# Moving softmax scaling, gate evictions and first taps between VectorE and ScalarE, and taking the recurrence's gates as a tangent of half the value, in a hybrid decoder step

## The chip, the core and the metric

The kernel runs on one core of a Trainium2 chip. Its engines are TensorE (PE, with its weight loads shown as PEld), VectorE (DVE), ScalarE (ACT), GpSimd (POOL) and SyncE (SP), which here issues the DMAs. The metric is device microseconds of one execution; the kernel before takes 1209.53 us (median of three runs, 1209.03 to 1210.03).

## The reference

One step of a hybrid decoder layer, for 1024 prompt tokens and 8 x 4 sample tokens, in float32. One input projection gives the columns of two groups. The recurrent group (RG-LRU, 512 features) goes through a convolution of width 4 over time, two block-diagonal gates and a linear recurrence; the attention group has 8 query heads and 2 key heads of width 64, a window of 128 and a learned sink per head. Both are normed, joined, projected, added to the input and layer-normed; a SwiGLU feed-forward (2816 wide) and a second layer norm follow.

```python
r = sigmoid(einsum(xb, w_a) + b_a);  i = sigmoid(einsum(xb, w_x) + b_x)
log_a = -8 * r * softplus(-lru_lambda)
a = exp(log_a)
u = sqrt(-expm1(2 * log_a)) * (i * x)
h = a * h + u                                  # over time
m = max(max(s), sink);  p = exp(s - m);  p = p / (sum(p) + exp(sink - m))
y_lru = gelu(gate) * lru_out
```

## The kernel before

All activations lie feature-major: 128 features on the partitions, tokens along the free axis, in two chunks of 512 and 544 tokens (the second is the last 512 prompt tokens and the 32 sample tokens, worked in two blocks of 272). Every float32 operand of a projection is split into a high and a low part, and a product takes three passes on TensorE (`three`, line 589).

The instructions are not issued in the order in which they are written. A recorder (`Recorder`) collects them, and a list scheduler (`order`, line 261) issues them per engine by the latest start that would not hold up TensorE, with a cost for each instruction worked out from its shape (`cost`, line 428). An instruction given to `either` may go to one of two engines: the first named does it if that is in time, otherwise the one that is through with it first (`leave`, line 313). `tt` (line 207) is such a choice between GpSimd and VectorE, `copy` (line 213) between ScalarE and VectorE. A function that needs another activation table than the one loaded is put back for a while (PATIENCE, line 62). All recorded instructions are issued from line 417, so the profile tells them apart by the names of their tiles.

The tiles that matter here:
- `attend` (line 849): one block of 128 queries for two heads. TensorE makes scores s; VectorE adds the mask and takes the minimum (p<-s,mk,ng); ScalarE takes the exponential of p with its sum in st; VectorE takes the reciprocal of st and scales p by it; TensorE transposes p into tp; ScalarE (or VectorE) copies tp to ph and VectorE makes the rest pl; TensorE multiplies with the values into o; ot and yat put the result together. `attend_sample` (line 905) does the same for the sample tokens, with pc for p.
- `recurrence` (line 1046): four taps over xr (and xe, the sample tokens) give xc; ps_g are the two gates' sums, which VectorE evicts to zz with the bias b_a or b_x.
- `scans` (line 1077): sigmoids of zz, then with L = -8 softplus(-lambda) r a tangent and an exponential; the products on zz, xc and hs; a square root; the scan over time into hs.
- `gate_stream` (line 1127): the gate branch; ps_gt is evicted to gt by VectorE.

The stages: up to about 42 us the loads and the first keys; to 473 us input projection, attention, recurrence, norms and output projection side by side, the projections filling TensorE between the steps of the other work; to 1190 us the feed-forward; then the last layer norm.

Of the kernel before, what the change touches and what calls it, by code (L numbers as in the profile page):

```python
# [12 lines left out]
F32 = mybir.dt.float32  # L13
# [39 lines left out]
# ---- a small list scheduler: the kernel below records its instructions; they are issued in the order in which they  # L53
# can run, given what each engine costs per instruction (shapes only), the data they wait for and the free buffers
# [9 lines left out]
TABLES = {"Sigmoid": "sigmoid", "Sqrt": "sqrt", "Gelu_apprx_tanh": "gelu", "Silu": "silu", "Exp": "exp"}  # L64


class RecordPool:
    """a tile pool whose tiles are made when their first instruction is issued; one opened late waits until all tiles
    of `behind` are done with"""
# [17 lines left out]
class Tag:  # L87
    def __init__(self, pool, kind, cap):
        self.pool, self.kind, self.cap, self.psum = pool, kind, cap, pool.psum
        self.bufs, self.free, self.first = [], cap, 0  # L90

# [58 lines left out]
class Recorder:  # L150
# [5 lines left out]
    def add(self, engine, fn, args, kw, *others):  # L156
        """`others`: (engine, function, args, kw) of instructions that would do the same on another engine"""
# [46 lines left out]
    def either(self, *calls):  # L204
        """an instruction that any of several engines can do: the one that would be through with it first"""
        self.add(*calls[0], *calls[1:])
# [9 lines left out]
    @contextlib.contextmanager  # L216
    def batch(self):
        """instructions that are to run one after the other: each waits for the data of all"""
        self.group = []
        yield  # L220
        waits = set().union(*(op.before for op in self.group)) - set(self.group)
        for op in self.group:
            op.before |= waits
        self.group = None

    def extra(self, b):
        """how many buffers the instructions recorded before b's may still need beside those in use"""
        t = b.tag
        ev = []
        for c in t.bufs[t.first : b.order]:  # L230
            if not c.taken:
                ev.append((c.start, 1))
                ev.append((c.end + 0.5, -1))
        ev.sort()
        n = peak = 0
        for _, d in ev:
            n += d
            peak = max(peak, n)
        return peak

    def deadlines(self):
        """op.key: the latest start that does not hold up the tensor engine, were it to run without a gap in the order
        of recording"""
# [19 lines left out]
    def order(self):  # L263
# [41 lines left out]
        def finish(op, e):  # L305
            """when engine e would be through with op after the more urgent work that waits for it"""
# [17 lines left out]
        def dispatch(e):  # L324
# [34 lines left out]
            for b in op.bufs:  # L359
                if not b.taken:  # L360
                    b.taken = True
                    t = b.tag
                    t.free -= 1
                    while t.first < len(t.bufs) and t.bufs[t.first].taken:
# [63 lines left out]
def cost(engine, fn, outs, ins, args, kw):  # L428
    """ns of an instruction, from its shape"""
# [23 lines left out]
def hybrid_step(ctx: ExitStack, tc: tile.TileContext, xT, w_in, w_gates, w_out, w_g, w_u, w_d, vec, ck, cv, ck_nat,  # L453
# [30 lines left out]
    # ---- constants and small vectors  # L484
# [13 lines left out]
    # ---- emission: a queue of matrix work fills the tensor engine between the steps of the other work  # L498
# [16 lines left out]
    def run_filler(stream, step):  # L515
        """emit the stream; after each `step` ns of its matmuls advance the other work"""
# [7 lines left out]
    # ---- weights: a unit is [128, 1024], split exactly into two float32r parts, prefetched in order of use  # L524
# [6 lines left out]
    def load(j):  # L531
        """raw halves of unit j"""
# [9 lines left out]
    def split_unit(j):  # L542
        if state["part"] == j and j < len(units):
# [9 lines left out]
            if halves:  # L553
                # less each row's mean over its columns: the second layer norm would take it off their sums
# [15 lines left out]
    def need(i):  # L570
        """unit i; at its first use the next unit is split and the one after that loaded"""
# [17 lines left out]
    def three(ps, n, wh, wl, xh, xl, start, stop):  # L589
        """(wh + wl).T @ (xh + xl) in three float32r passes"""  # L590
# [5 lines left out]
    def block(ps, u, xs, o, n, kts=range(KT)):  # L596
        """one [128, n] block of a projection: unit u against feature-major activations xs"""
# [7 lines left out]
    # ---- start: the first tokens and the key and value weights arrive and are split tile by tile  # L605
    def wake():
        """while the first loads are on their way: the exponential's table, and the tensor engine's clock"""
# [76 lines left out]
    # 8 * softplus(-lambda) = 8 * (max(-lambda, 0) + log1p(exp(-|lambda|))), the log1p by its atanh series  # L684
    sp = const.tile([P, 8, 4], F32, tag="sp", name="sp")
    lam = vec_cols("lam", 0, 4)
    e_, s_, s2, poly, sp8, nsp8, ab, _ = (sp[:, i] for i in range(8))
# [4 lines left out]
    bcen = ng2[:, 0:8]  # L692
    def small_vectors():
        # b_out less its mean over the features
# [7 lines left out]
        # -sink for the running minimum, and the query bias with the (negated) attention scale  # L702
# [16 lines left out]
        nc.vector.scalar_tensor_tensor(sp8, poly, 2.0, ab, op0=ALU.mult, op1=ALU.add)  # L719
        nc.vector.tensor_scalar(sp8, sp8, 8.0, None, op0=ALU.mult)  # L720
        nc.vector.tensor_scalar(nsp8, sp8, -1.0, None, op0=ALU.mult)

    # ---- rotary embedding
# [7 lines left out]
    # ---- keys and values of token chunk s  # L731
# [4 lines left out]
    def key_stack(g, s, kraw):  # L736
        """[k; k] of a key group, in two float32r parts"""
# [810 lines left out]
```

## Time and profile before

| | us |
|---|---|
| median of the runs | 1209.53 |
| profiled execution, first to last instruction (span) | 1207.1 |
| TensorE busy | 1147.1 (95%) |
| VectorE busy | 631.5 (52%) |
| ScalarE busy | 431.3 (36%) |
| GpSimd busy | 491.1 (41%) |

The page gives for the profiled execution its span; the median of the runs stands 2.4 us above it. The shares are means over the stages named above, which differ: they are to be read stage by stage. Busy time of one engine can overlap at the seams of two instructions; a wait is put down to the instruction that ended it.

### The profile page before, as it was taken

How to read it: one execution, taken by the hardware profiler on the slowest of the kernel's cores; microseconds unless marked ns; L12 is line 12 of the kernel's file. 1: busy time of each engine (PE TensorE's matmuls, PEld its weight loads, DVE VectorE, ACT ScalarE, POOL GpSimd, SP SyncE). 2: the span in 40 equal slices, each digit the busy share in tenths (PEclk: the TensorE clock that was granted, in tenths of full speed). 3: DMA queues.
4: the chain of work that ended last, by engine and by line, in shares of the span. 5: the costliest groups of instructions: out<-in, count | busy, mean ns of one | idle time of the engine just before them, and what ended most of it. 6: DMA issues, size and time to landing. Idle time of an engine off the chain costs nothing.

```text
span 1207.1 us, 18093 instructions
## 1 busy us (share of the span) xinstructions
PE 1147.1 (95%) x7024; PEld 1023.9 (85%) x7024; DVE 631.5 (52%) x1259; ACT 431.3 (36%) x878; POOL 491.1 (41%) x493
## 2 busy tenths in 40 slices
PE   9788998788888999999999999999999999999996
PEld 7568898776668979999898998989999899999986
DVE  5999889899977577252324142232415132232135
ACT  5375666567545375311120212113021211202135
POOL 6843476666556978412031222203031221303241
PEclk9899999899989999999999999999999999999998
DMA  8410113243121223211011111111111110202004
GB/s 291 136 53 19 41 49 101 65 142 117 63 89 54 80 78 129 90 36 53 26 63 35 53 53 45 44 36 53 36 65 41 53 44 27 70 19 70 1 1 144
DMA packets 48085, 80.42 MB, mean 67 GB/s; under 512 B 8144, under 2 KB 12400, under 8 KB 47984
## 3 DMA queue, kind: packets, MB, share of 16 engines
q1 hardware_dynamic: 48000, 79.27, 19.8%
q8 instruction: 55, 0.90, 0.3%
q14 instruction: 30, 0.25, 0.1%
HBM read 71.98 MB, written 5.58 MB: 64 GB/s over the span
## 4 chain that ended last, share of the span: by engine, by line
PE 73%; DVE 17%; DMA 3%; issue 2%; ACT 2%; POOL 2%; SPq 1%; DVEq 0%; POOLq 0%; ACTq 0%
PE ps_d L417 21%; PE ps_fg L417 20%; PE ps_fu L417 20%; PE ps_o L417 4%; DVE p L417 3%; PE ps_gt L417 3%; DVE xc L417 2%; DVE y L417 1%; DVE yat L417 1%; DVE qst L417 1%; SPq L417 1%; DVE hs L417 1%; DVE pl L417 1%; DMA x_r<-in_dram 1%; DVE v L417 1%
## 5 line engine op out<-in xcount | busy, mean ns | idle before, releaser
L417 POOL TENSOR_TENSOR wg_l<-wg_r,wg_h 128x512 fp32r<-128x512 f32 x50 | 64.8, 1311 | 344.4 <-ACT wg_h L417 344.4
L417 DVE SCALAR_TENSOR_TENSOR y<-y,ps_d 128x272 f32<-128x272 f32 (+1 forms) x240 | 124.9, 521 | 107.2 <-PE ps_d L417 102.5
L417 PE MATMUL ps_fg<-h_h,wg_l 128*128 128x272 f32 (+1 forms) x528 | 171.7, 325 | 0.4 <-POOL wg_l L417 0.4
L417 PE MATMUL ps_fg<-h_h,wg_h 128*128 128x272 f32 (+1 forms) x528 | 171.6, 325 | 0.0
L417 PE MATMUL ps_fg<-h_l,wg_h 128*128 128x272 f32 (+1 forms) x528 | 171.4, 325 | 0.0
L417 PE MATMUL ps_d<-hid_h,wd_l 128*128 128x272 f32 (+1 forms) x528 | 171.3, 325 | 0.0
L417 DVE TENSOR_REDUCE wd_c<-wd_r 128x1 f32<-128x512 f32 x44 | 30.0, 682 | 269.3 <-DMA wd_r<-in_dram 269.3
L417 PE MATMUL ps_fu<-h_h,wu_l 128*128 128x272 f32 (+1 forms) x528 | 170.7, 323 | 0.0
L417 PE MATMUL ps_fu<-h_h,wu_h 128*128 128x272 f32 (+1 forms) x528 | 170.6, 323 | 0.0
L417 PE MATMUL ps_d<-hid_h,wd_h 128*128 128x272 f32 (+1 forms) x528 | 170.6, 324 | 0.0
L417 PE MATMUL ps_d<-hid_l,wd_h 128*128 128x272 f32 (+1 forms) x528 | 170.4, 324 | 0.0
L417 PE MATMUL ps_fu<-h_l,wu_h 128*128 128x272 f32 (+1 forms) x528 | 170.4, 323 | 0.0
L417 POOL TENSOR_TENSOR hid_l<-sg,hid_h 128x272 fp32r<-128x272 f32 (+1 forms) x66 | 63.3, 960 | 126.0 <-ACT hid_h L417 108.3
L417 ACT ACTIVATE sg<-ps_fg 128x272 f32<-128x272 f32 (+1 forms) x66 | 30.5, 463 | 232.4 <-PE ps_fg L417 232.4
L417 PEld LDWEIGHTS ps_fg<-h_h,wg_l 128*128 128x128 f32 x528 | 99.8, 189 | 8.5 <-POOL wg_l L417 0.6
L417 PEld LDWEIGHTS ps_fg<-h_l,wg_h 128*128 128x128 f32 x528 | 99.5, 189 | 7.9
L417 PEld LDWEIGHTS ps_fg<-h_h,wg_h 128*128 128x128 f32 x528 | 99.8, 189 | 7.7
L417 PEld LDWEIGHTS ps_d<-hid_h,wd_l 128*128 128x128 f32 x528 | 99.2, 188 | 8.2 <-issue 0.2
L417 PEld LDWEIGHTS ps_d<-hid_h,wd_h 128*128 128x128 f32 x528 | 99.2, 188 | 8.0 <-issue 0.2
L417 PEld LDWEIGHTS ps_fu<-h_l,wu_h 128*128 128x128 f32 x528 | 99.3, 188 | 7.8
L417 PEld LDWEIGHTS ps_d<-hid_l,wd_h 128*128 128x128 f32 x528 | 99.2, 188 | 7.9
L417 PEld LDWEIGHTS ps_fu<-h_h,wu_l 128*128 128x128 f32 x528 | 99.3, 188 | 7.7
(346 smaller groups left out, 2553.1 us busy)
## 6 DMA issues: line engine op xcount, KB each, us to landing
wg_r<-in_dram SPq DMA_DIRECT2D x50, 256.0 KB, 2.6
wu_r<-in_dram SPq DMA_DIRECT2D x50, 256.0 KB, 2.6
wd_r<-in_dram SPq DMA_DIRECT2D x44, 256.0 KB, 2.6
wo_r<-in_dram SPq DMA_DIRECT2D x32, 256.0 KB, 2.6
wq_r<-in_dram SPq DMA_DIRECT2D x16, 256.0 KB, 3.6
wx_r<-in_dram SPq DMA_DIRECT2D x12, 256.0 KB, 3.5
x_r<-in_dram SPq DMA_DIRECT2D x8, 272.0 KB, 4.6
y<-in_dram SPq DMA_DIRECT2D x8, 272.0 KB, 3.4
```

What stands on the lines that cost most here:

```text
L417: getattr(getattr(self.nc, op.eng), op.fn)(*[real(a) for a in op.args], **{k: real(v) for k, v in op.kw.items()})
```

## The change

Five edits, all ahead of the feed-forward:
- The scaling of p and pc by the reciprocal becomes a choice: ScalarE first, VectorE otherwise (`scaled`).
- The first tap of the convolution, and the eviction of ps_gt, become such a choice too.
- The two gates are evicted from PSUM by ScalarE as tanh(x/2 + b/2), with halved biases hb. As sigmoid(x) = (1 + tanh(x/2)) / 2, the separate sigmoids go; tangent and exponential of L take their missing half from a bias, with 4 softplus in place of 8.
- i * x becomes (i' + 1) * x in one VectorE instruction, where it was a product that GpSimd or VectorE could do, and the missing factor 1/2 goes into the square root as scale 0.25.
- u * sqrt(...) now names GpSimd first where it named VectorE first. The table list gets Tanh under "exp", so that the scheduler counts a tangent as belonging to the exponential's table.

The remaining lines of the diff rewrite `extra` to the same result and drop comments. The core:

```diff
-TABLES = {"Sigmoid": "sigmoid", ..., "Silu": "silu", "Exp": "exp"}
+TABLES = {"Sigmoid": "sigmoid", ..., "Silu": "silu", "Exp": "exp", "Tanh": "exp"}
...
+        nc.vector.tensor_scalar(hbias, vec_cols("b_a", 0, 8), 0.5, None, op0=ALU.mult)
...
+    def scaled(p, r):
+        nc.either(("scalar", "activation", (p, p, AF.Identity), dict(scale=r)),
+                  ("vector", "tensor_scalar", (p, p, r, None), dict(op0=ALU.mult)))
...
-            nc.vector.tensor_scalar(pr[:, j, 8 : 8 + w], pr[:, j, 8 : 8 + w], st[:, 4 + j : 5 + j], None, op0=ALU.mult)
+            scaled(pr[:, j, 8 : 8 + w], st[:, 4 + j : 5 + j])
...
-            nc.vector.tensor_scalar(pc[i], pc[i], st[:, 7:8], None, op0=ALU.mult)
+            scaled(pc[i], st[:, 7:8])
...
-            nc.vector.tensor_scalar(dst, src(0), tap[0], col("conv_b", j), op0=ALU.mult, op1=ALU.add)
+            nc.either(("scalar", "activation", (dst, src(0), AF.Identity), dict(scale=tap[0], bias=col("conv_b", j))),
+                      ("vector", "tensor_scalar", (dst, src(0), tap[0], col("conv_b", j)),
+                       dict(op0=ALU.mult, op1=ALU.add)))
...
-                nc.vector.tensor_scalar(zz[q][:, o : o + m], ps[:, :m], col(bias, j), None, op0=ALU.add)
+                nc.scalar.activation(zz[q][:, o : o + m], ps[:, :m], AF.Tanh, bias=hbias[:, 4 * q + j : 4 * q + j + 1],
+                                     scale=0.5)
...
-        with nc.batch():
-            for i in items:
-                nc.scalar.activation(gr[i], gr[i], AF.Sigmoid)
-                nc.scalar.activation(gi[i], gi[i], AF.Sigmoid)
...
-            nc.scalar.activation(t2[i], gr[i], AF.Tanh, scale=sp8[:, i[0] : i[0] + 1])
-        for i in items:
-            nc.tt(gi[i], gi[i], cut(xcs[i], i[1]), op=ALU.mult)
-            nc.scalar.activation(gr[i], gr[i], AF.Exp, scale=nsp8[:, i[0] : i[0] + 1])
+            c = slice(i[0], i[0] + 1)
+            nc.scalar.activation(t2[i], gr[i], AF.Tanh, scale=sp4[:, c], bias=sp4[:, c])
+            nc.scalar.activation(gr[i], gr[i], AF.Exp, scale=nsp4[:, c], bias=nsp4[:, c])
+            nc.vector.scalar_tensor_tensor(gi[i], gi[i], 1.0, cut(xcs[i], i[1]), op0=ALU.add, op1=ALU.mult)
...
-                nc.scalar.activation(t2[i], t2[i], AF.Sqrt)
+                nc.scalar.activation(t2[i], t2[i], AF.Sqrt, scale=0.25)
...
-            nc.tt(u, u, h, op=ALU.mult, first="vector")
+            nc.tt(u, u, h, op=ALU.mult)
...
-                nc.vector.tensor_scalar(graw[j, s][:, o : o + n], ps[:, :n], col("b_in", 4 + j), None, op0=ALU.add)
+                g = graw[j, s][:, o : o + n]
+                nc.either(("scalar", "activation", (g, ps[:, :n], AF.Identity), dict(bias=col("b_in", 4 + j))),
+                          ("vector", "tensor_scalar", (g, ps[:, :n], col("b_in", 4 + j), None), dict(op0=ALU.add)))
```

As the costs and choices feed the scheduler, instructions move on every engine. Two places show it. In names such as p_1_0 the first number is the query tile and the second the block; ISA is VectorE's mask-and-minimum or the read of its result.

VectorE, at blocks 0_3 to 1_1 of the first chunk, before:

```order
L417 RECIPROCAL st_0_3_795<-st_0_3_795 128x2
L417 TENSOR_SCALAR p_0_3_365<-p_0_3_365,st_0_3_795 128x256 x2
L417 TENSOR_TENSOR yat00_766<-o_0_2_846,ot_0_2_868 64x128 x2
L417 RECIPROCAL st_1_0_844<-st_1_0_844 128x2
L417 ISA p_1_1_761,st_1_1_896<-s_1_1_876,mk_272,ng_257 128x256
L417 ISA st_1_1_896 128x1
L417 TENSOR_SCALAR p_1_0_712<-p_1_0_712,st_1_0_844 128x128 x2
```

The same engine and blocks, now:

```order
L418 RECIPROCAL st_1_0_855<-st_1_0_855 128x2
L418 TENSOR_TENSOR pl_0_3_898<-tp_0_3_871,ph_0_3_887 128x512
L418 TENSOR_TENSOR qst40_894<-q20raw_727,qst40_894 64x512
L418 SCALAR_TENSOR_TENSOR hs10_683<-xc10_584,hs10_683 128x512
L418 ISA p_1_1_765,st_1_1_928<-s_1_1_905,mk_274,ng_257 128x256
L418 ISA st_1_1_928 128x1
```

The four scalings have left this stretch, and a product of the recurrence (hs10) that came later has moved in.

ScalarE, at the same blocks, before (zz are the gates, which are brought through the sigmoid between two table loads):

```order
L417 ACT_TABLE_LOAD
L417 ACTIVATE zz000_524<-zz000_524 128x512
L417 ACTIVATE zz100_659<-zz100_659 128x512
L417 ACTIVATE zz101_682<-zz101_682 128x512
L417 ACTIVATE zz001_544<-zz001_544 128x512
L417 CAST ph_0_2_836<-tp_0_2_805 128x512
L417 ACT_TABLE_LOAD
L417 ACTIVATE p_0_3_365,st_0_3_795<-p_0_3_365,st_0_3_795 128x257 x2
L417 COPY ot_0_2_868<-o_0_2_846 64x256
L417 ACTIVATE p_1_0_712,st_1_0_844<-p_1_0_712,st_1_0_844 128x129 x2
```

And now:

```order
L418 CAST ph_0_2_823<-tp_0_2_812 128x512
L418 ACTIVATE p_0_3_367,st_0_3_804<-p_0_3_367,st_0_3_804 128x257 x2
L418 ACTIVATE p_0_3_367<-p_0_3_367,st_0_3_804 128x256 x2
L418 ACTIVATE p_1_0_740,st_1_0_855<-p_1_0_740,st_1_0_855 128x129 x2
L418 COPY ot_0_2_879<-o_0_2_862 64x256
L418 CAST ph_0_3_887<-tp_0_3_871 128x512
L418 CAST qst40_894<-q20raw_727 64x512
L418 ACTIVATE p_1_0_740<-p_1_0_740,st_1_0_855 128x128 x2
L418 CAST qst50_914<-q20raw_727 64x512
L418 CAST wx30_h_922<-wx30_r0_670 128x512
```

The table loads and the sigmoids are gone from here; the scaling of block 0_3 stands right behind its exponential, that of block 1_0 four rows behind, and copies and weight casts stand behind them.

## Rows read from the trace of the kernel before

**Rows 1.** Busy time of the engines in stages: from:to and length in us, then busy us and instructions of PE, PEld, DVE, ACT, POOL, the granted clock as a share of 2.4 GHz, the DMA share and GB/s.

```profile
42.00:145.00 103.00, 88.50 (x505) 74.09 (x504) 98.02 (x234) 54.62 (x139) 48.17 (x62) 0.93 0.13 39
145.00:190.00 45.00, 45.00 (x297) 41.41 (x296) 33.13 (x49) 32.78 (x53) 33.12 (x35) 1.00 0.19 62
190.00:345.00 155.00, 132.40 (x817) 114.56 (x817) 143.65 (x320) 95.96 (x213) 98.36 (x98) 0.94 0.33 103
345.00:395.00 50.00, 44.20 (x275) 39.27 (x274) 37.72 (x62) 24.34 (x44) 32.01 (x25) 0.90 0.16 53
395.00:473.00 78.00, 75.54 (x454) 66.27 (x452) 56.40 (x110) 42.41 (x89) 69.20 (x66) 0.98 0.25 85
473.00:1190.00 717.00, 717.00 (x4493) 652.98 (x4494) 225.06 (x428) 147.35 (x281) 176.70 (x159) 1.00 0.14 48
```

**Rows 2.** TensorE's waits from 42 to 395 us, longest first: who waited for whom, us in total, times, longest us.

```profile
PE tp L417 <- DVE p L417: 12.1, 12, 3.6
PE ps_g L417 <- ACT xc_h L417: 3.4, 1, 3.4
PE ps_g L417 <- DVE q21raw L417: 3.0, 1, 3.0
PE n_b L417 <- DVE n_d L417: 2.6, 1, 2.6
PE s L417 <- DVE qst L417: 2.2, 2, 1.8
```

**Rows 3.** The page's part 1 (busy us, share and instructions of each engine) and the first line of part 4 (the chain of waits that ended last, by engine, as shares of the span), then the same chain by line, from its own view.

```profile
PE 1147.1 (95%) x7024; PEld 1023.9 (85%) x7024; DVE 631.5 (52%) x1259; ACT 431.3 (36%) x878; POOL 491.1 (41%) x493
...
PE 73%; DVE 17%; DMA 3%; issue 2%; ACT 2%; POOL 2%; SPq 1%; DVEq 0%; POOLq 0%; ACTq 0%
...
by line: PE ps_d L417 21.1%; PE ps_fg L417 19.7%; PE ps_fu L417 19.6%; PE ps_o L417 4.4%; DVE p L417 3.4%; PE ps_gt L417 3.2%; issue 2.0%; DVE xc L417 1.9%; DVE y L417 1.4%; DVE yat L417 1.0%; DVE qst L417 1.0%; SPq L417 1.0%; DVE hs L417 0
```

**Rows 4.** Groups of VectorE's instructions over the whole span, each shape apart: operation, output<-inputs, shape, count, busy us, mean ns of one, idle us before them.

```profile
L417 DVE TENSOR_SCALAR p<-p,st 128x256 f32<-128x256 f32 x56 | 34.2, 647 | 0.1
L417 DVE CUSTOM_DVE_ANT_0 p<-s,mk,ng 128x256 f32<-128x256 f32 x56 | 25.5, 474 | 0.8 <-PE s L417 0.7
...
L417 DVE TENSOR_SCALAR zz<-ps_g,vt 128x272 f32<-128x272 f32 x16 | 7.8, 491 | 0.1
...
L417 DVE TENSOR_SCALAR xc<-xr,vt 128x512 f32<-128x512 f32 x8 | 7.2, 902 | 1.5 <-ACT xr L417 1.4
...
L417 DVE TENSOR_SCALAR zz<-ps_g,vt 128x512 f32<-128x512 f32 x8 | 6.0, 744 | 0.1
...
L417 DVE SCALAR_TENSOR_TENSOR hs<-xc,hs 128x544 f32<-128x544 f32 x4 | 4.1, 1052 | 0.1
...
L417 DVE TENSOR_TENSOR gt<-gt,gt 128x544 f32<-128x544 f32 x3 | 3.8, 1277 | 0.0
L417 DVE TENSOR_TENSOR zz<-zz,hs 128x544 f32<-128x544 f32 x4 | 3.8, 976 | 0.0
...
L417 DVE TENSOR_SCALAR pc<-pc,sts 128x512 f32<-128x512 f32 x4 | 3.0, 745 | 0.0
...
L417 DVE SCALAR_TENSOR_TENSOR hs<-xc,hs 128x512 f32<-128x512 f32 x4 | 2.7, 682 | 0.0
L417 DVE TENSOR_TENSOR zz<-zz,hs 128x512 f32<-128x512 f32 x4 | 2.7, 690 | 0.0
L417 DVE CUSTOM_DVE_ANT_0 p<-s,mk,ng 128x128 f32<-128x128 f32 x8 | 2.5, 345 | 0.0
...
L417 DVE TENSOR_SCALAR xc<-xe,vt 128x32 f32<-128x32 f32 x4 | 2.1, 534 | 0.0
...
L417 DVE TENSOR_SCALAR p<-p,st 128x128 f32<-128x128 f32 x8 | 1.9, 280 | 0.0
...
L417 DVE COPY ot<-o 64x256 f32<-64x256 f32 x2 | 0.9, 426 | 0.1
```

**Rows 5.** VectorE's instructions on the tile p from 42 to 395 us: count, duration in ns (shortest/median/longest), first and last start in us, shapes.

```profile
L417 DVE CUSTOM_DVE_ANT_0 p<-s,mk,ng x64: 335/473/484, 59.3 to 325.6; 128x256 f32<-128x256 f32 x56, 128x128 f32<-128x128 f32 x8
L417 DVE TENSOR_SCALAR p<-p,st x64: 267/348/1455, 61.3 to 332.2; 128x256 f32<-128x256 f32 x56, 128x128 f32<-128x128 f32 x8
```

**Rows 6.** VectorE and GpSimd in order of time, a piece at 83 to 87 us: start us, us, instruction, count.

```profile
84.38 2.19 DVE L417 TENSOR_SCALAR p<-p,st 128x256 f32<-128x256 f32 x2
...
83.42 3.00 POOL L417 TENSOR_TENSOR wx_l<-wx_r,wx_h 128x512 fp32r<-128x512 f32 x2
```

**Rows 7.** Groups of ScalarE's instructions over the whole span, columns as in rows 4.

```profile
L417 ACT ACTIVATE p<-p,st 128x257 f32<-128x257 f32 x56 | 28.2, 505 | 6.4 <-DVE st L417 6.3
L417 ACT ACT_TABLE_LOAD x21 | 26.9, 1283 | 1.1 <-PEq L1526 0.7
...
L417 ACT COPY ot<-o 64x256 f32<-64x256 f32 x30 | 11.1, 369 | 15.6 <-PE o L417 15.1
...
L417 ACT ACTIVATE y<-y,vt 128x512 f32<-128x512 f32 x8 | 6.0, 806 | 5.6 <-DVE y L417 5.6
...
L417 ACT ACTIVATE zz<-zz 128x544 f32<-128x544 f32 x8 | 4.7, 646 | 0.0
...
L417 ACT ACTIVATE p<-p,st 128x129 f32<-128x129 f32 x8 | 3.2, 397 | 5.9 <-DVE st L417 5.9
...
L417 ACT ACTIVATE xr<-ps_x,vt 128x512 f32<-128x512 f32 x4 | 2.7, 684 | 0.1
...
L417 ACT ACTIVATE xr<-ps_x,vt 128x272 f32<-128x272 f32 x4 | 2.0, 489 | 1.6 <-PE ps_x L417 1.6
```

**Rows 8.** From the waits of all engines over the whole span: ScalarE's for the sums and minima st.

```profile
ACT p L417 <- DVE st L417: 12.2, 10, 5.9
```

More of the change, by code (lines that the diff above doesn't have):

```diff
@@ L63 @@
 TURNS = ("mm", "s", "tp", "o", "wh", "wl", "wr")
-TABLES = {"Sigmoid": "sigmoid", "Sqrt": "sqrt", "Gelu_apprx_tanh": "gelu", "Silu": "silu", "Exp": "exp"}
+TABLES = {"Sigmoid": "sigmoid", "Sqrt": "sqrt", "Gelu_apprx_tanh": "gelu", "Silu": "silu", "Exp": "exp", "Tanh": "exp"}
 class RecordPool:
@@ L90, in __init__ @@
         self.bufs, self.free, self.first = [], cap, 0
+        self.peaks = None
 class Buf:
@@ L228, in extra @@
         t = b.tag
-        ev = []
-        for c in t.bufs[t.first : b.order]:
+        if t.peaks is None:
+            t.peaks = (t.first, [0], [])
+        base, peaks, ends = t.peaks
+        for c in t.bufs[base + len(peaks) - 1 : b.order]:
             if not c.taken:
[L232 to L239, printed above, removed]
+                while ends and ends[0] < c.start:
+                    heapq.heappop(ends)
+                heapq.heappush(ends, c.end)
+            peaks.append(max(peaks[-1], len(ends)))
+        return peaks[max(b.order - base, 0)]
     def deadlines(self):
@@ L363, in dispatch @@
                     t.free -= 1
+                    t.peaks = None
                     while t.first < len(t.bufs) and t.bufs[t.first].taken:
@@ L686, in hybrid_step @@
     lam = vec_cols("lam", 0, 4)
-    e_, s_, s2, poly, sp8, nsp8, ab, _ = (sp[:, i] for i in range(8))
+    e_, s_, s2, poly, sp4, nsp4, ab, _ = (sp[:, i] for i in range(8))
     ng = const.tile([P, 16], F32, tag="ng", name="ng")
@@ L692, in hybrid_step @@
     bcen = ng2[:, 0:8]
+    hbias = const.tile([P, 8], F32, tag="hb", name="hb")
     def small_vectors():
@@ L718, in small_vectors @@
         nc.vector.tensor_scalar(ab, lam, -1.0, 0.0, op0=ALU.mult, op1=ALU.max)
-        nc.vector.scalar_tensor_tensor(sp8, poly, 2.0, ab, op0=ALU.mult, op1=ALU.add)
-        nc.vector.tensor_scalar(sp8, sp8, 8.0, None, op0=ALU.mult)
-        nc.vector.tensor_scalar(nsp8, sp8, -1.0, None, op0=ALU.mult)
+        nc.vector.scalar_tensor_tensor(sp4, poly, 2.0, ab, op0=ALU.mult, op1=ALU.add)
+        nc.vector.tensor_scalar(sp4, sp4, 4.0, None, op0=ALU.mult)
+        nc.vector.tensor_scalar(nsp4, sp4, -1.0, None, op0=ALU.mult)
+        nc.vector.tensor_scalar(hbias, vec_cols("b_a", 0, 8), 0.5, None, op0=ALU.mult)
     def swap_halves(sw, raw, n):
@@ L1067, in recurrence @@
         gh, gl = gate_weights(j)
-        for q, bias in enumerate(("b_a", "b_x")):
+        for q in range(2):
             for b, (o, m) in enumerate(BL[s]):
```

## The prediction

> **What bounds the kernel now.** I read the busy shares by stage first [rows 1]. The reader is to see three regimes. From 473 us to 1190 us TensorE is busy in every microsecond, at full clock, while VectorE has a third of the time: nothing done for VectorE or ScalarE there can shorten anything, and the diff has no edit there. From 145 to 190 us TensorE is just as full (45.0 of 45). But from 42 to 145 us and from 190 to 345 us VectorE is the full engine: 98.0 of 103 us (95%) and 143.7 of 155 us (93%), with TensorE idle for 14.5 and 22.6 us and its granted clock at 0.93 and 0.94, which means that it ran at the lower of its two levels (1.2 GHz) for about an eighth of these stages. ScalarE is busy 53% and 62% there. From 345 to 473 us TensorE is idle for 8.3 us.
>
> Next, what TensorE waits for in 42 to 395 us [rows 2]: the longest entry is the transposes (tp) that wait for VectorE's probabilities p, 12.1 us in 12 waits, and most others shown end on VectorE too (qst, q21raw, n_d). Last, the chain of waits [rows 3]: VectorE holds 17% of the span, 205 us; "DVE p" alone is 3.4%, 41 us. The busy time of all instructions that this can be is 34.2 + 25.5 + 2.5 + 1.9 = 64.1 us [rows 4], so 0.64 of the work on p stands on the chain that sets the end.
>
> **VectorE's account.** By the issue order, 40 of 64 scalings of p leave VectorE: 33 of 256 columns x 647 ns = 21.4 us, 7 of 128 x 280 ns = 2.0 [rows 4]. All 24 evictions of the gates' sums leave: 16 x 491 + 8 x 744 ns = 13.8. Eleven of 12 evictions of ps_gt, by the same rows: 7 x 491 + 4 x 744 = 6.4. Eleven of 12 first taps of the convolution: 7 x 902 + 4 x 534 = 8.4. The four scalings of pc: 3.0. To GpSimd go seven products zz<-zz,hs (4 x 690 + 3 x 976 = 5.7) and four sums of squares (4 x 1277 = 5.1), and one more product (976) becomes part of a new form. Sum 66.8 us. Added: eight fused (i+1)*x, which this trace lacks; the same instruction over the same sizes without a pointer is hs<-xc,hs, 4 x 682 + 4 x 1052 ns = 6.9; six copies ot, 6 x 426 = 2.6; one small vector 0.2; and nine more moves that the order shows, net, at the 690 ns of a 512-column product, 6.2. Net 66.8 - 15.9 = **51 us less on VectorE**.
>
> The bound from below: the scaling of 256 columns has 348 ns as median and 1455 ns as longest, while the masking instruction, which reads PSUM, stays within 335 to 484 [rows 5]. The long ones lie beside GpSimd: at 84.38 us two of them take 2.19 us while GpSimd runs wx_l [rows 6]. If that waiting merely moves to the next VectorE instruction, the 33 are worth 348 ns each and the net is 41 us. I take 51, since an instruction on ScalarE is not there to collide, and keep 41 for the range. The Trainium skill (SBUF — State Buffer, "SBUF: two separate sides") calls the port pair of VectorE and GpSimd an exclusive lock that VectorE's two-input instructions also meet; by that the next one inherits the wait, and the sum below would be about 5 us less gain. The long cases beside wx_l agree with the lock; no row shows the inheriting.
>
> Where these 51 us fall, by the names of the tiles. In 42 to 145 us: 12 + 7 scalings (9.8), 11 gate evictions (7 x 744 + 4 x 491 = 7.2), 4 + 2 first taps (4.7), less four copies ot and some work that now comes earlier (two fused products, two more of the recurrence's products and two scans, which stood after 145 us): about 14 us. In 190 to 345 us: 21 scalings (13.6), 8 gate evictions (3.9), 2 + 2 taps (2.9), pc (3.0), sums and products (6.0), less about 6.5 added: about 23 us. The remaining 14 us leave the stretch 145 to 190 us, where TensorE has no gap, and are worth nothing.
>
> How much of the 37 us passes on? At most 0.95 of it, if a full queue simply gets shorter; at the lower end VectorE's share of the chain over its busy time in 42 to 473 us, 205 us less some 10 for head and tail, so about 195 of 369 us, 0.53 [rows 1, 3]. I take the 0.64 of the p rows, since p is the largest part: **-24 us**. TensorE's idle time in the two stages is 37 us, so it can be had. Gaps that close also give back clock: 0.07 x 103 + 0.06 x 155 = 16.5 us are lost at most, if TensorE is what is waited for all that time. In these stages it mostly is not, so of the bounds, nothing and two thirds (11 us), I take a value near the lower: -2 us.
>
> **ScalarE's account.** Added: 24 gate evictions with the tangent (16 x 489 + 8 x 684, the rows of xr, which have a pointer bias and read PSUM) 13.3; 40 scalings, by the exponential over the same columns (33 x 505 + 7 x 397) 19.4; ps_gt by the same rows (7 x 489 + 4 x 684) 6.2; taps, 7 x 806 by a row with two pointers and 4 short ones at 397, 7.2; pc 4 x 684 = 2.7. Sum 48.8 us [rows 7]. Gone: 16 sigmoids at 646, 10.3; five of 21 table loads, 5 x 1283 = 6.4; six copies ot, 6 x 369 = 2.2. Net **+30 us**. In 42 to 395 us that raises it from 208 to about 238 of 353 us [rows 1]. It costs at least nothing, while its idle time covers it, at most all 30 if every addition is on the path; ScalarE holds 2% of the chain (24 us of its 250 busy us in 42 to 473 us [rows 1, 3]), so a tenth: **+3 us**. If that cover is gone, what is queued behind a waiting scaling on ScalarE is the copy ph of the next block and the weight casts wgt_h and wo_h, which GpSimd and then TensorE wait for. GpSimd gets one instruction less in number; I cost it at nothing: 63% busy in the fuller of the two stages [rows 1]. The order of TensorE's matmuls is nearly the same, their number the same.
>
> The Trainium skill (ScalarE: Activation LUTs, "Rules for kernel authors") tells to multiply on VectorE and not on ScalarE. The median of VectorE's scaling, 348 ns, against 505 ns for ScalarE's exponential over one column more, agrees with it for one instruction alone; 40 x 0.16 us = 6 us if all of it were on the path, and the time would be 1193.
>
> **Sum.** -24 - 2 + 3 = -23 us on the profiled span of 1207.1 us, 1184. The median of the runs is 1209.53, 2.4 us above that span, so 1186.5; I say 1186.
>
> **Rivals.** (a) More: both stages are simply as long as VectorE's queue; 0.95 x 37 = 35, and two thirds of the 16.5 us of clock, 11, less 3 on ScalarE: -43, 1167. For it: 95% and 93% busy. Against: such a gain would need more than all the 37 us of TensorE's idle time together with faster matmuls, and chains such as n_t to n_d (2.6 us [rows 2]) have a latency that no queue explains.
> (b) Little: VectorE's queue shortens but the gaps stay, since they end on single chains (norms, rotated queries, DMA); only the p waits, 12.1 us, halve: -6, 1203. For it: no single entry but p is above 3.5 us [rows 2]. Against: nearly all of them stand on VectorE, and behind its queue.
> (c) Slower: ScalarE issues in order, and 29 blocks now have a scaling in its queue that waits for VectorE's reciprocal, mostly one to five rows behind the block's own exponential. ScalarE's waits for st cost it 12.2 us in 10 times so far [rows 8], 1.2 us each. If each of the 29 blocks adds 1.2 us and all of it reaches TensorE through ph and the weight casts, 35 us stand against 23 saved: 1221; the change turns to a loss from 0.8 us a block on. For it: 62% busy, with stretches that are full. Against: ScalarE would have 115 us idle in 353, and the planner puts other instructions between exponential and scaling in most blocks.
> (d) The change hardly does what it says: where either engine may scale, 24 of 64 stay on VectorE, and nothing outside p matters: within 0.2%.
>
> **Chances.** Forecast, 1175 to 1198: 0.60. (a), 1158 to 1175: 0.12. (b), 1198 to 1207: 0.11. (d), within 0.2% of 1209.5, about what a measurement of this kernel can tell from no change: 0.05. (c), above 1212: 0.12. So faster 0.83, same 0.05, slower 0.12. The forecast's own ends come from the bounds: 41/51 x 37 x 0.53 = 16 us, less 3 on ScalarE, is -13, 1196; 35 and 2 less 3 is -34, 1175. The range 1164 to 1210 leaves out a third of (a) below, (c) and a little of (d) above, 0.18 together; the ScalarE bound, all 30 us against 26 saved, is 1213 and lies in (c).
>
> **What would show it.** Right: VectorE's busy time near 580 us in all and ScalarE's near 461 (631.5 and 431.3 before [rows 3]); sixteen table loads; the wait of tp for DVE p mostly gone from TensorE's list; TensorE's stretch without a gap, which began at about 473 us, begins near 450; granted clock in the stages before it above 0.95; the part after it as long as before, 717 us. Wrong: waits of TensorE for ACT p, ph or wo_l that take the place of DVE p (c); TensorE's idle time before the gapless part still above 35 us with VectorE well under 85% busy (b).

## The result and the profile after

The changed kernel takes 1200.66 us (median of four runs, 1198.41 to 1202.54) beside 1209.62 for the kernel before on the same chip: ratio 0.9930, 95% interval 0.9911 to 0.9948. That is 8.5 us, where the forecast said 23; the sign is right, and the time lies in the range but not in the forecast's own band (1175 to 1198). The profiled execution, the fastest of the four, took 1198.41 us, with a span of 1196.6.

Part 1 of the page, as in [rows 3]:

```profile
PE 1141.1 (95%) x7024; PEld 1022.3 (85%) x7024; DVE 595.8 (50%) x1181; ACT 454.3 (38%) x937; POOL 484.8 (41%) x492
```

The same stages as in [rows 1], with the same columns:

```profile
42.00:145.00 103.00, 90.03 (x529) 77.86 (x528) 91.27 (x207) 79.58 (x188) 51.32 (x67) 0.97 0.14 45
145.00:190.00 45.00, 44.03 (x297) 40.53 (x297) 22.76 (x32) 23.23 (x40) 28.27 (x31) 1.00 0.19 60
190.00:345.00 155.00, 136.09 (x831) 118.60 (x831) 130.90 (x307) 106.80 (x244) 95.17 (x98) 0.93 0.33 100
345.00:395.00 50.00, 46.12 (x324) 42.57 (x323) 32.92 (x47) 22.93 (x40) 39.10 (x34) 0.97 0.23 74
395.00:473.00 78.00, 74.91 (x449) 65.79 (x448) 58.03 (x108) 44.25 (x92) 66.67 (x63) 0.98 0.30 92
473.00:1190.00 717.00, 713.10 (x4457) 648.18 (x4456) 226.62 (x432) 148.50 (x282) 170.93 (x154) 1.00 0.15 47
```

VectorE lost 35.7 us in all (631.5 to 595.8). In the stages in which TensorE has gaps, 42 to 145 and 190 to 473 us, it lost 335.8 - 313.1 = 22.7 us (the four rows added, before less after). In the two stages that were full it lost 6.8 and 12.8 us, 19.5 together, where the forecast had 14 and 23; 10.4 us left the stage from 145 to 190 us. VectorE is still 89% and 84% busy in the two full stages. ScalarE rose to 77% in the first. The span's 10.5 us come from two sources: TensorE's idle time fell from 60.0 to 55.5 us (span less busy), and its 7024 matmuls themselves took 6.0 us less (1147.1 to 1141.1).

TensorE's waits from 42 to 395 us, to be read beside [rows 2]:

```profile
PE s L418 <- DVE qst L418: 5.7, 3, 3.9
PE tp L418 <- ACT p L418: 5.2, 4, 2.5
PE tp L418 <- DVE p L418: 5.0, 6, 1.9
PE o L418 <- DVE pl L418: 3.7, 4, 1.6
PE n_b L418 <- DVE n_d L418: 3.5, 2, 3.3
```

The wait for p has not gone: 12.1 us in 12 times for VectorE's p became 10.2 us in 10 times for p on either engine. One of them, in order of time (start us, us, engine, instruction, in brackets the idle time before it and what ended it):

```profile
80.69 1.65 DVE L418 TENSOR_TENSOR qst<-q20raw,qst 64x512 fp32r<-64x512 f32 x1
...
82.37 1.66 DVE L418 TENSOR_TENSOR q30sw<-q30sw,rope 128x512 f32<-128x512 f32 x1
...
83.95 0.15 DVE L418 RECIPROCAL st<-st 128x2 f32<-128x2 f32 x1
84.14 0.51 ACT L418 ACTIVATE p<-p,st 128x256 f32<-128x256 f32 x1 [2.11 <-DVE st L418]
84.14 0.35 DVE L418 TENSOR_SCALAR p<-p,st 128x256 f32<-128x256 f32 x1
...
84.70 0.52 PE L418 MATMUL tp<-oi,p 128*128 128x128 f32 x2 [1.84 <-ACT p L418]
```

ScalarE was free from 82.03 us on, but the reciprocal that its scaling waits for stands in VectorE's queue behind two products of the queries. Moving the scaling away leaves the block's chain tied to VectorE by the instruction ahead of it.

### The profile page after: what moved, and what is told of

Its sections match the earlier page's. It is cut to its first block, busy times and chain, and to the rows that moved or that the text cites. A ratio compares the mean times of both kernels' runs of the same rounds, so it can differ in the third digit from the quotient of the medians.

```text
span 1196.6 us, 18012 instructions
## 1 busy us (share of the span) xinstructions
PE 1141.1 (95%) x7024; PEld 1022.3 (85%) x7024; DVE 595.8 (50%) x1181; ACT 454.3 (38%) x937; POOL 484.8 (41%) x492
## 4 chain that ended last, share of the span: by engine, by line
PE 68%; DVE 4%; ACT 1%; issue 0%; POOL 0%; DMA 0%; DVEq 0%; POOLq 0%; ACTq 0%
PE ps_d L418 21%; PE ps_fg L418 20%; PE ps_fu L418 20%; PE ps_o L418 5%; DVE y L418 1%; DVE v L418 1%; DVE h_l L418 1%; PE v_b L418 0%; DVE v_d L418 0%; PE ps_var L418 0%; DMA wu_r<-in_dram 0%; PE v_t L418 0%; PE ps_m L418 0%; DVE p L418 0%; ACT q L418 0%
## 5 line engine op out<-in xcount | busy, mean ns | idle before, releaser
L418 PEld LDWEIGHTS ps_fu<-h_h,wu_h 128*128 128x128 f32 x528 | 99.2, 188 | 7.8
```

The costliest lines, as they stand in the source:

```text
L418: getattr(getattr(self.nc, op.eng), op.fn)(*[real(a) for a in op.args], **{k: real(v) for k, v in op.kw.items()})
```

## The experiments

Each ratio is against the kernel before on the same chip, with its 95% interval; microseconds of gain are the ratio times 1209.5. "VectorE in the stages" is its busy time in 42 to 145 and 190 to 473 us, as added above.

### The parts alone, each planned anew

Three kernels take over one part of the diff each: `scaled` for p and pc; the gates as tangents with all that belongs to them (halved biases, no sigmoids, the fused product, GpSimd first for u); the first taps and the eviction of ps_gt.

> The kernel before with the scaling of p and pc as a choice, and nothing else changed. Three theories. Queue (the one on record): 41 scalings and four of pc leave VectorE, some 29 us by the rows, all in the two full stages; 0.64 of that less 3 on ScalarE is -15 us, 1194. Chain: TensorE's gaps end on the block chains (mask, exponential, reciprocal, scaling, transpose) in the planned order, and the queue was full partly with work done ahead of need, so a microsecond off VectorE is worth about 0.25: -5 to -8, 1202 to 1205. ScalarE: its added 23 us, with no table load saved here, take the gain away: 1208 or more.

> The kernel before with the gates evicted by ScalarE as tangents, the sigmoids gone, the fused product and GpSimd first for u; p, pc, the first taps and ps_gt stay on VectorE. Queue: about 12 us off VectorE in the two stages, less some 6 us added there, 0.64 of it, and five table loads less: -5 us, 1204. Chain: no block's chain is shortened, within 3 us of before. ScalarE: as good as alone responsible for the gain, since table loads and sigmoids leave it: -7 or more, 1202.

> The kernel before with the first taps and the eviction of ps_gt as choices, nothing else. Queue: about 8 us off VectorE where it counts, 0.64 of it, 1204. Chain: within 3 us of before, since these stand in no block's chain. ScalarE: 13 us more on it for nothing, 1211.

Measured: scaling alone 0.9966 (0.9947 to 0.9984), -4.1 us; gates alone 0.9984 (0.9971 to 0.9997), -1.9; taps and ps_gt alone 1.0015 (1.0005 to 1.0024), +1.8. VectorE fell by 6.5, 10.1 and 11.3 us (625.0, 621.4, 620.2). The first of these says little of what left VectorE, 41 scalings of p and two of pc: it holds one sum of 8.78 us, which waits beside GpSimd (shown at the end). The time does not follow VectorE's total: with 11.3 us less the third part is slower. Nor does it follow TensorE's waits for p, 8.9, 17.9 and 6.6 us in the three parts. Each of these numbers also holds a new order, whose own price comes next.

### Other orders of the same instructions

The planner's latency between engines, set to 190 and to 210, in the kernel before and in the changed one:

```diff
-LATENCY = 200.0
+LATENCY = 190.0
```

> The kernel before planned with a latency of 190 in place of 200 ns between engines; the same instructions in a somewhat other order. If the plan's order itself decides a few microseconds: 3 us or more beside before, either way. If not: within 2 us.

> The kernel before planned with a latency of 210 in place of 200 ns. If the plan's order itself decides a few microseconds: 3 us or more beside before, either way, and not the mirror image of 190. If not: within 2 us.

> The changed kernel planned with a latency of 190 in place of 200 ns. If the order that a plan happens to have decides some microseconds whatever the instructions: 3 us or more beside the changed kernel's 1200. If the changed kernel's order is a poor draw among its like: 1195 or less. If its time is set by chains that any order has: 1198 to 1203.

> The changed kernel planned with a latency of 210 in place of 200 ns. The same three cases: 3 us or more beside 1200; 1195 or less; 1198 to 1203. With the run at 190 it gives three orders of the changed kernel beside three of the kernel before (1204, 1208, 1216): if the change is worth what the prediction said, the mean of three is some 20 us lower; if only what the one pair showed, some 9.

Kernel before: 0.9965 (0.9954 to 0.9977) and 1.0066 (1.0049 to 1.0084), -4.2 and +8.0 us, with no instruction added or taken away but where the planner may choose an engine. VectorE's time in the stages goes along (322.9, 335.8 and 338.4 us at 190, 200 and 210), and so does TensorE's wait for VectorE's p: 9.8, 12.1 and 14.2 us. Changed kernel: 0.9921 (0.9902 to 0.9940) and 0.9938 (0.9924 to 0.9951), beside 0.9930 at 200; there the waits for p differ (5.5, 10.2 and 6.2 us on both engines) where the times are not told apart. So the changed kernel's order is no poor draw, and the mean of three orders gives (-9.6 - 8.5 - 7.5 + 4.2 + 0 - 8.0) / 3 = -9.8 us for the change, near what the one pair showed and far from 23. The parts alone lie within such draws and are not told apart.

### The order held, only the scaling touched

To keep the planner out, the following kernels use the order of the kernel before as it is and change instructions only when they are issued: the scaling is left out, or goes to ScalarE, or is replaced by a sum of the same columns that nobody reads:

```diff
         for op in self.order():
+            if op.fn == "tensor_scalar" and op.args[0].buf is op.args[1].buf and op.args[0].buf.name[:2] in ("p_", "pc"):
+                continue
...
+                op.eng, op.fn, op.args, op.kw = "scalar", "activation", (*op.args[:2], AF.Identity), dict(scale=op.args[2])
...
+                self.nc.vector.reduce_sum(junk[:, 0:1], real(op.args[1]), axis=mybir.AxisListType.X)
+                continue
```

Left out:

> The kernel before in its own planned order, with all scalings of p and pc left out when the instructions are issued (the probabilities stay unnormed; everything else is computed). Nothing comes in their place on ScalarE. Queue: 39 us off VectorE by the rows, 0.64 of it, -25 us, 1185. Chain: only the waits of the transposes for p (12.1 us) go for the most part, -8 to -12, 1198 to 1201. On the port that VectorE shares with GpSimd: if the waiting of long scalings is their own, VectorE's busy time falls by 39 us to 592; if the next instruction inherits it, by 64 times the median of about 0.35 us, some 23, to 608.

On ScalarE:

> The kernel before in its own planned order, with all 64 scalings of p and the four of pc issued by ScalarE at the place where VectorE had them. Fixed order: the move itself is worth what leaving the scalings out was worth (-18 us) but for one hop between engines, -13 to -18, 1190 to 1195; what the change made of it (-4 with p alone, -9 in all) was lost in planning anew. ScalarE: 35 us of scalings in order behind exponentials hold up its copies and casts, 1203 or more. Record's sum: 39 us by the rows x 0.64, less 5, -20.

One of each pair on ScalarE:

> The kernel before in its own planned order, the first scaling of each pair issued by VectorE, the second by ScalarE, at the place where both were. Chain: the two halves run side by side, so the step in each block's chain is one scaling instead of two; of the 11 us between scaling on ScalarE (1201) and no scaling (1190) about half comes, 1194 to 1198, faster than with all 64 on either engine. VectorE's time alone at 0.25: half of 8 us, 1205. ScalarE's in-order queue: between the two whole cases, 1203 to 1207.

Load kept, but beside the chain:

> The kernel before in its own planned order; in the place of each scaling of p and pc VectorE sums the same columns into a spare column that nobody reads (the probabilities stay unnormed). VectorE keeps some 64 x 0.35 + 4 x 0.68, 25 us of load, but no transpose waits for it. Chain: of the 18.7 us that leaving out brought, the 9 that VectorE's load does not explain come, 1198 to 1201. Load: nothing comes but the difference between 25 and 39 us at 0.4, 1203 to 1208. If a load at that place holds up the next step as much as the scaling did: 1207 or more.

Left out: 0.9845 (0.9833 to 0.9858), -18.7 us. On ScalarE: 0.9935 (0.9920 to 0.9949), -7.9. Split: 0.9953 (0.9935 to 0.9971), -5.7, not the expected gain over both whole cases. Beside the chain: 0.9959 (0.9945 to 0.9972), -5.0, as the load explanation had it and not the 9 us of the chain. VectorE's part 1 and TensorE's longest waits from 42 to 395 us, first with the scaling left out:

```profile
PE 1137.9 (96%) x7024; PEld 1020.5 (86%) x7024; DVE 605.8 (51%) x1191; ACT 430.6 (36%) x878; POOL 490.8 (41%) x493
...
PE o L419 <- ACT ph L419: 4.7, 3, 3.4
PE ps_g L419 <- ACT xc_h L419: 2.7, 1, 2.7
```

with all of it on ScalarE:

```profile
PE 1144.3 (95%) x7024; PEld 1021.0 (85%) x7024; DVE 598.9 (50%) x1191; ACT 457.9 (38%) x946; POOL 489.8 (41%) x493
...
PE tp L419 <- ACT p L419: 10.8, 12, 3.8
```

with VectorE's sums beside the chain, and the sums as a group (count, busy us, mean ns):

```profile
PE 1143.4 (95%) x7024; PEld 1024.4 (85%) x7024; DVE 623.4 (52%) x1259; ACT 431.1 (36%) x878; POOL 489.1 (41%) x493
...
PE o L423 <- ACT ph L423: 6.1, 2, 3.3
...
L417 DVE TENSOR_REDUCE junk<-p 128x1 f32<-128x256 f32 x56 | 23.2, 414 | 1.0
```

The second fence is the heart of the case. VectorE is relieved of 32.6 us, 27.5 of them in the stages, where the whole change takes 22.7, and the transposes wait for p as often and almost as long as before, now on ScalarE (10.8 us in 12 times beside 12.1 in 12 [rows 2]). Taking the step out of the chain and keeping a load (third fence) ends that wait, as in the first fence (the longest is then for ScalarE's copy ph), and gives 5.0 us, with 9.3 us of VectorE's time in the stages gone as well; taking load away and keeping the step gives 7.9; both together give 18.7, more than the sum of 12.9. This reads as two limits side by side, VectorE's load and the blocks' chains, where relief of one alone is partly hidden by the other. One rival is left: with all scalings on ScalarE that engine has 26.6 us more to do (431.3 to 457.9), and what this costs in this order was not measured by itself.

### VectorE's load where no block chain is touched

```diff
         for op in self.order():
+            if op.fn == "scalar_tensor_tensor" and op.args[0].buf.name[:2] == "xc" and op.args[3].buf is op.args[0].buf:
+                continue
```

> The kernel before in its own planned order, with taps two to four of the convolution left out when the instructions are issued (36 instructions on VectorE, 24 x 996 ns and 12 x 354 ns, 28 us; the recurrent branch then goes on with the first tap alone). No block chain gets shorter and ScalarE gets nothing. Price 0.64, the record's: -18, 1191. Price 0.25: -7, 1202. If only block chains count: the single wait for xc_h (3.4 us) at most, 1206 to 1209.

> The changed kernel in its own planned order, with taps two to four of the convolution left out (36 instructions on VectorE, 24 x 1010 ns and 12 x 556 ns, 31 us). If VectorE's time still sets the end at 0.64: -20, 1180. At 0.25: -8, 1192. If after the change VectorE is no bound any more: within 3 us of 1200.

Kernel before: 0.9929 (0.9909 to 0.9949), -8.6 us for 335.8 - 313.8 = 22.0 us less on VectorE in the stages, 0.39 each. Changed kernel: 0.9832 (0.9809 to 0.9854), 0.0098 below the changed kernel, -11.8 us for 313.1 - 290.8 = 22.3, 0.53 each. The four stages of the first and then of the second, with columns as in [rows 1]:

```profile
42.00:145.00 103.00, 89.49 (x542) 77.18 (x542) 82.70 (x214) 62.79 (x151) 51.14 (x66) 0.97 0.16 47
190.00:345.00 155.00, 135.16 (x817) 116.45 (x818) 135.46 (x324) 93.57 (x211) 94.47 (x98) 0.94 0.32 100
345.00:395.00 50.00, 45.35 (x329) 42.84 (x329) 34.42 (x47) 22.66 (x39) 38.79 (x33) 0.97 0.20 64
395.00:473.00 78.00, 71.60 (x423) 62.32 (x422) 61.18 (x110) 44.03 (x92) 62.88 (x60) 0.98 0.28 90
```

```profile
42.00:145.00 103.00, 95.83 (x572) 84.05 (x571) 79.38 (x195) 83.28 (x196) 55.70 (x70) 0.97 0.17 50
190.00:345.00 155.00, 140.46 (x855) 121.86 (x856) 123.21 (x294) 106.64 (x242) 97.11 (x100) 0.94 0.33 100
345.00:395.00 50.00, 46.45 (x345) 44.31 (x344) 31.85 (x51) 21.21 (x37) 39.69 (x35) 0.97 0.23 74
395.00:473.00 78.00, 75.11 (x449) 65.89 (x448) 56.34 (x105) 47.80 (x99) 63.42 (x61) 0.98 0.31 100
```

These prices are rough. The intervals of the ratios alone leave 0.28 to 0.50 for the first and some 0.37 to 0.69 for the second, so the two are not told apart. In the first, 5.8 us of VectorE's time are one instruction that waits beside GpSimd (shown at the end); without it 27.8 us went, 0.31 each. By the added durations that the expectations used, 28 and 31 us, the prices are 0.31 and 0.38, well below 0.64; the first cannot be told from 0.25.

No attention block is touched, but the taps have a place of their own on the chain that ended last: "DVE xc" with 1.9% of the span, 23 us [rows 3], of some 37 us of work on xc. That share is 0.6, like the 0.64 of p, and the measured price is lower.

The wait for p of the first, with the line of part 1:

```profile
PE 1136.5 (95%) x7024; PEld 1018.2 (85%) x7024; DVE 611.1 (51%) x1223; ACT 431.0 (36%) x878; POOL 485.0 (40%) x493
...
PE tp L419 <- DVE p L419: 11.5, 12, 3.6
```

Some 22 us off VectorE's queue leave the wait for p where it was, 11.5 us in 12 times. So in this order it does not hang on the queue's total, which points to the blocks' chains.

### The changed kernel's own order

The same edits on the changed kernel: ScalarE's scalings back on VectorE at the same place; ScalarE's scalings left out; all scalings left out.

> The changed kernel in its own planned order, with the 40 scalings of p and four of pc that went to ScalarE issued by VectorE at the same place of the order. Queue: 27 us come back on VectorE, 0.64 of it, +16 or more, 1216. Chain: VectorE's shorter scaling against ScalarE's, one hop between engines less, some more queueing: +3 to +8, 1204 to 1208. ScalarE: its relief by 22 us shows, 1200 or less.

> The changed kernel in its own planned order, with the 40 scalings of p and four of pc that ScalarE does left out when the instructions are issued (those probabilities stay unnormed). Queue: VectorE's work is the same, so within 3 us of the changed kernel, 1198 to 1201. Chain: 5.2 us that the transposes wait for ScalarE's p, and half a microsecond in some blocks where the wait is for VectorE's next step: -4 to -7, 1194 to 1197. ScalarE: 22 us off the engine that was 89% busy from 90 to 145 us, -10 or more, 1190.

> The changed kernel in its own planned order, with all 64 scalings of p and four of pc left out on both engines (the probabilities stay unnormed). Leaving out ScalarE's alone changed nothing (1198). Load: the 24 on VectorE, 14 us by the rows, at 0.4 to 0.5, -6 to -7, 1192 to 1194. Chain: the transposes' 10.2 us of waits for p go as well, 1188 to 1191, where the kernel before without scaling stands (1190): then the rest of the change is worth nothing beside it.

Back on VectorE: 1.0058 (1.0035 to 1.0081), 15.5 us slower than the changed kernel (0.0128 of 1209.5), for 26.4 us more on VectorE (622.2). That is 0.59 each, near what the queue's theory expected, though some 8 of the 26.4 are again one sum that waits beside GpSimd (8.73 us). ScalarE's left out: 0.9924 (0.9906 to 0.9942), the same as the changed kernel. All left out: 0.9862 (0.9843 to 0.9881), -8.2 us against it; the kernel before without scaling stands at 0.9845, so there the rest of the change is worth nothing. The waits of the first and of the second of these:

```profile
PE tp L420 <- DVE p L420: 16.1, 15, 2.8
```

```profile
PE tp L420 <- DVE p L420: 9.1, 8, 2.7
```

With ScalarE relieved of 18.9 us (454.3 to 435.4), TensorE waits for VectorE's p 9.1 us instead of 5.0: it seems that what ScalarE's wait had covered comes up elsewhere. ScalarE's scalings cost nothing that can be told in this order. Putting them back costs more than the whole change gained, so the gain is no property of the diff alone. A likely reason, not tested by itself: an order that was planned with VectorE relieved has filled its queue with other work, and the scaling then waits behind it (16.1 us in 15 times).

### Two attempts at a faster version

> The same substitution in the order that was planned with a latency of 190 (1204 without it). Fixed order: the two gains add, 1204 less 13 to 18, 1186 to 1191, faster than both kernels. If that order was quick because it already avoided the waits for p, or if ScalarE holds: 1198 or more.

> The changed kernel with the first scaling of each pair always on VectorE and the second always on ScalarE (pc likewise), planned with a latency of 190. Chain: shorter steps in all blocks, 1192 to 1196, faster than both kernels and than the changed one at 190 (1198). If the planner's choice of 40 was already as good: 1197 to 1201. If ScalarE's queue or more load on VectorE counts: 1202 or more.

Scaling on ScalarE in the order of 190: 0.9948 (0.9936 to 0.9960), no gain over that order alone (0.9965) that can be told; that order already had shorter waits for p (9.8 us), which may be why. The split pairs at 190: 0.9945 (0.9933 to 0.9958), in the last of the three cases (1202 or more), with 9.8 us of waits for VectorE's p. The best, the changed kernel planned at 190 (0.9921), cannot be told from the changed kernel.

## Why the prediction was right in sign and wrong in size

**VectorE's account, 51 us of which 37 count.** This step failed first. The instructions counted were right: with the durations of the kernel before, what left VectorE comes to 71.8 us and what came to 22.2, net 49.6 (66.8 and 15.9 were forecast). Three things stand between that and the 22.7 us that count. First, instructions that stayed grew longer, 4.9 us net (count times mean, all groups). The groups of VectorE and then of ScalarE, whole span, with columns as in [rows 4]:

```profile
L418 DVE TENSOR_SCALAR p<-p,st 128x256 f32<-128x256 f32 x23 | 13.7, 603 | 0.3
...
L418 DVE TENSOR_TENSOR_SCAN hs<-zz,zz 128x512 f32<-128x512 f32 x4 | 7.1, 1786 | 0.0
L418 DVE SCALAR_TENSOR_TENSOR xc<-xe,vt,xc 128x32 f32<-128x32 f32 x12 | 6.7, 556 | 0.1
...
L418 DVE SCALAR_TENSOR_TENSOR zz<-zz,xc 128x512 f32<-128x512 f32 x4 | 3.5, 872 | 0.1
L418 DVE COPY ot<-o 64x256 f32<-64x256 f32 x8 | 3.4, 427 | 2.3 <-PE o L418 2.1
L418 DVE SCALAR_TENSOR_TENSOR zz<-zz,xc 128x544 f32<-128x544 f32 x4 | 2.8, 710 | 0.0
```

```profile
L418 ACT ACT_TABLE_LOAD x16 | 20.5, 1283 | 1.0 <-PEq L1535 0.7
L418 ACT ACTIVATE p<-p,st 128x256 f32<-128x256 f32 x33 | 16.1, 505 | 8.9 <-DVE st L418 8.6
...
L418 ACT ACTIVATE zz<-ps_g,hb 128x272 f32<-128x272 f32 x16 | 7.4, 488 | 0.1
```

The taps of 32 columns went from 354 ns before to 556, the scans of 512 from 1479 to 1786, each with the same count; other groups got shorter. What was added came out as forecast: the fused products at 872 and 710 ns, 6.3 us (6.9 said), and six more copies ot at 427. Second, neighbours on an engine overlap in the rows: in the trace above 82.37 + 1.66 is 84.03, and the next instruction starts at 83.95. The durations (count times mean) sum to 44.7 us less, part 1 to 35.7; the 9.0 us between them are overlaps that went with the 78 instructions fewer, 0.12 each. The prediction added durations and did not take that off. Third, 35.7 less 22.7 fell elsewhere, 10.4 of it from 145 to 190 us (14 forecast). There VectorE now stands idle:

```profile
162.25 1.29 DVE L418 TENSOR_TENSOR_SCAN hs<-zz,zz 128x544 f32<-128x544 f32 x1 [0.36 <-POOL zz L418]
180.31 1.30 DVE L418 TENSOR_TENSOR hs<-hs,gt 128x512 f32<-128x512 f32 x2 [16.77 <-ACT gt L418]
```

So the 37 us of the prediction that count were 22.7, and 19.5 in the two stages for which it counted them. By its own factor of 0.64, 22.7 us would be worth 14.5 us instead of 23.7: taken first, this term accounts for 9 of the 14.5 us that were missed.

**The bound from below, the inherited wait.** The prediction took the scalings at their mean, with the median as the other end. In the held order the mean was right: with all scalings on ScalarE the durations of VectorE's instructions sum to 41.6 us less, and those of p and pc, count times mean, come to 41.5 [rows 4]; 68 seams at 0.13 make of that the 32.6 us of part 1. The Trainium skill (SBUF — State Buffer, "SBUF: two separate sides") calls the port pair that VectorE and GpSimd share an exclusive lock. That the next instruction then inherits the wait, as the prediction read it, does not show there. With the scalings left out VectorE fell by only 25.7 us, to 605.8, near the 608 that was expected if the wait is inherited; but some 7 us of the difference are again seams, 5.9 are one instruction far behind the scalings, shown at the end, and only 2.9, net, are other instructions that grew longer. The 4.9 us of longer instructions appear in the changed kernel with its new order; what lengthened them stays open.

**The pass-on factor, 0.64.** This step failed next. It took the share of the work on p that stands on the chain of waits for the price of a microsecond anywhere on VectorE. Measured on the taps, outside the attention blocks, the price is 0.39 in the old order and 0.53 in the new (0.31 and 0.38 by added durations); 22.7 x 0.39 = 8.9, close to what the change gave. That it comes so close is partly luck: planned at 190 and at 210 the change takes 16.8 and 24.6 us off VectorE in the stages and gains 5.3 and 15.5 us, 0.32 and 0.63 each (0.47 at 210 without a long wait that stands in the changed kernel's VectorE time there, shown at the end). A share of the chain tells that the step was the last to end, not what comes second: with p's wait shortened, qst and n_d came to 5.7 and 3.5 us (2.2 and 2.6 before [rows 2]). And the largest part of what the change moves, the scaling, is on a chain that it leaves as long, or longer: ScalarE's scaling took 505 ns, as forecast, beside VectorE's median of 348.

**The clock, -2.** Too low: matmuls took 6.0 us less, more than the idle time fell (4.5). The granted clock, 0.978 in the mean before and 0.982 after, rose from 0.93 to 0.97 in the first stage and from 0.90 to 0.97 in 345 to 395 us, but went from 0.94 to 0.93 in 190 to 345; above 0.95 was forecast.

**ScalarE, +3.** 454.3 us (461 forecast) with sixteen table loads, as said, and the gates' tangents at 488 ns (489 forecast). The run without its scalings, 18.9 us less on ScalarE, shows no price that can be told (0.9924 beside 0.9930); the gates, the taps and ps_gt on ScalarE were not priced by themselves. Of the Trainium skill's advice (ScalarE: Activation LUTs, "Rules for kernel authors") to multiply on VectorE, the 6 us worked out in the prediction do not show: here the faster engine is the fuller one, and putting the scalings back on it cost 15.5 us.

**The signs.** VectorE near 580: 595.8. The wait for VectorE's p mostly gone: it halved, and ScalarE's p took its place, as rival (c) has it for a sign, but without its loss. TensorE without a gap from 450 us: from 463. The part behind it as long as before: it began 10 us earlier (473 to 463), and the last matmul of ps_fg came 10.5 us earlier (1131.6 to 1121.1). TensorE idle above 35 us before the gapless part, rival (b)'s sign, came true (431 less 391.2 busy, 39.8 us, beside 45.4), while VectorE was not well under 85%. The result is in (b)'s band (1198 to 1207), which had a chance of 0.11; its mechanism, gaps that end on single chains, has its part in it, and its p waits did halve on VectorE, but it left out that ScalarE took the other half over. Rival (a) would have needed the full queue to be the only limit.

**What stays open.** Why the split pairs gave no more than 5.7 us, although they shorten the step; why a given relief comes now as less idle time, now as faster matmuls; and what the scalings cost ScalarE in the old order, without which the two limits are the likely reading and not a shown one.

## What to carry to other kernels

A full engine and a chain through it are two limits: ask of each moved instruction whether the step leaves the chain or only changes engine, and price the relief by leaving out work beside that chain, in the order that is held fixed, since a share of the chain of waits is no price. Count busy time from the page and not from added rows, only in stages where the bound engine has gaps, and look for single records that hold a long wait. Where a scheduler orders the work, plan it also with a constant slightly off, before a few microseconds are put down to an edit.

## What the runs showed of the hardware that was not expected

One VectorE instruction can wait through a whole series of GpSimd's. In the kernel before without the taps, h_l took 6.52 us on VectorE. Beside it GpSimd ended one product and did five more instructions without a gap, until 404.30 us; h_l ended at 404.85 (start us, us, engine, instruction):

```profile
396.05 2.56 POOL L419 TENSOR_TENSOR h_l<-y,h_h 128x512 fp32r<-128x512 f32 x2
...
398.33 6.52 DVE L419 TENSOR_TENSOR h_l<-y,h_h 128x512 fp32r<-128x512 f32 x1
398.56 1.28 POOL L419 TENSOR_TENSOR wg_l<-wg_r,wg_h 128x512 fp32r<-128x512 f32 x1
399.80 3.77 POOL L419 TENSOR_TENSOR h_l<-y,h_h 128x512 fp32r<-128x512 f32 x3
403.53 0.77 POOL L419 TENSOR_TENSOR sum<-sum,y 128x272 f32<-128x272 f32 x1
```

In the kernel before the same instruction took 0.68 us: GpSimd had paused for 0.23 us ahead of wg_l. The long wait came in the run without scaling too (6.54 us), and makes up 5.9 us there that the scalings left behind. A sum over 272 columns, 0.43 us where it is short, did the same in three other runs: with scaling alone (8.78 us, from 398.45 to 407.23; GpSimd's series ended at 406.93), in the changed kernel at 210 (8.85) and in the changed kernel with the scalings back on VectorE (8.73). The wait counts as busy time, so VectorE's totals of these five runs hold 6 to 8 us that are no work:

```profile
398.45 8.78 DVE L417 TENSOR_TENSOR sum<-sum,y 128x272 f32<-128x272 f32 x1
...
403.15 3.78 POOL L417 TENSOR_TENSOR h_l<-y,h_h 128x512 fp32r<-128x512 f32 x3
```

The other surprise is the matmuls' own time. Without the taps TensorE's idle time did not fall at all (span 1197.6 less 1136.5 busy is 61.1 us, 60.0 before); the whole gain is 10.6 us less for the same 7024 matmuls, with the granted clock at 0.985 in the mean, beside 0.978.
